# First modulation vectors and sum of squares computed on TensorE instead of VectorE and GpSimd, and six later modulation pieces issued at other places

## The chip, the cores and the metric

The kernel runs on one core of one Trainium2 chip. The core has five engines with their own instruction streams: PE (TensorE, matrix products), ACT (ScalarE), DVE (VectorE), POOL (GpSimd) and SP (SyncE, which here only issues loads and stores). They meet at semaphores. The metric is the time of one execution on the device, in microseconds (us), lower is better.

## The reference

Two small transformer blocks of two layers each run on one sequence `x` of 256 tokens with 1024 features. What the change touches is the start of the first layer: a condition vector `c` gives six modulation vectors, and the first two of them shift and scale the normed input.

```python
mod = jax.nn.silu(c) @ ada_w + ada_b                    # c (1, 1024), ada_w (1024, 6144)
sh_m, sc_m, gt_m, sh_f, sc_f, gt_f = jnp.split(mod[:, None, :], 6, axis=-1)
h = rms_norm(x, norm_mix) * (1 + sc_m) + sh_m
(aq, ak, av, bq, bkc, bvc, ..., cqkv, cz, ca, cb) = jnp.split(h @ w_in, points, axis=-1)
o_a = banded_attention(...)                             # four heads, window 128
o_b = nsa_mixer(...)                                    # compressed, selected and window branches
o_c = gated_delta_net(...)                              # short convolution, then a scan over chunks
x = x + gt_m * (jnp.concatenate([o_a, o_b, o_c], axis=-1) @ w_out)
h = rms_norm(x, norm_ffn) * (1 + sc_f) + sh_f
gate, up = jnp.split(h @ w_gate_up, 2, axis=-1)
x = x + gt_f * ((silu(gate) * up) @ w_down)
```

`rms_norm` divides each token by the root of its mean square, so it needs a sum of squares over all 1024 features of a token.

## The kernel before

Activations lie feature-major: `x` is a tile of 128 partitions by 8 feature blocks (k = 0 to 7) by 256 tokens. Every product with a weight is done as three products in a reduced 32-bit type. `cut` (L188) splits a weight tile into a high part `wh` (a cast on ACT, L193) and a low part `wl` (a subtraction, L194, on DVE or on POOL where `eng` says so). The activations are split in the same way into `hh` and `hl`, and `mm3` (L207 to 211) issues high by high, low by high and high by low.

`begin0` (L452) is the start. It loads `c` and `x`, spreads `c` over all partitions by a product with ones (`cb`, L465), and squares the eight blocks of `x` on ACT (L65) while POOL adds the squares up (L67, one chain of seven). Two products with a column of ones then give the sums (`nps`, L81), `rstd` and `spread` turn them into `rb`, a tile that holds 1/rms of each token on every partition (two products, L272, and a copy, L472). Then four steps j follow. Each takes two modulation units (`mod_unit`, L339), splits one weight block of 512 KB, norms two feature blocks and adds the products that have become possible into four results `pf`.

A modulation unit loads 1 MB, two rows of 1024 weights per partition; DVE multiplies each with the spread silu(c) and sums it (L346), adds the bias (L349) and, for a scale, multiplies the norm's gain in (L352). Units 0 to 3 are the shift, 4 to 7 the scale: eight units, sixteen sums. `norm` (L298) does, for each feature block, `h` = x times `rb` on POOL (L303), scale and shift on ACT (L305), a cast on ACT (L308) and `hl` on POOL (L309).

Units 8 to 23 of layer 0 wait in `pump_list`. `pump(n)` (L355) takes n of them off at fixed places in `mixer1` (L498), in the order of the program. Weights and units come through one ring of three buffers (tag "ws"; `begin0` has five of its own for units), and all their loads stand in the one queue of SP, in order. A load whose buffer is not free holds up all loads behind it.

In `mixer1` the results of the first four blocks go into the convolution, then come `pm`, the query and key blocks, the solve of the delta net, the compression, the loop over `aq` blocks, weight blocks 4 to 7 (`conv(4, ...)`), the loop over `bq` blocks, weight blocks 8 to 11, the gate product `pz`, and the scan (`gdn_scan`), whose first product is `qp`.

Of the kernel before, what the change touches and what calls it, by code (L numbers as in the profile page):

```python
# [17 lines left out]
P = 128  # L18
S = 256
# [123 lines left out]
class Net:  # L143
# [307 lines left out]

    def begin0(self, w_fm, pp):  # L452

        nc, tc, io = self.nc, self.tc, self.io
        with tc.tile_pool(name="st", bufs=1) as sp:
            row = sp.tile([1, 1024], F32, name="row")
            nc.sync.dma_start(row, io["c"])
            nc.sync.dma_start(self.x, io["x"])
            nc.sync.dma_start(self.adab, io["ada_b"])
            nc.sync.dma_start(self.nrm, io["norms"])  # L460
            nc.sync.dma_start(self.cw, io["gdn_conv_w"])
# [10 lines left out]
            nc.scalar.copy(self.rb[:, 0:S], self.spread(self.rcol, (pp, "s", 2)))  # L472
            out = [self.pj.tile([P, S], F32, tag="pj", name="pf") for _ in range(2)]
            out += [pp.tile([P, S], F32, tag="g", name="pf", bufs=3) for _ in range(2)]
            w = []
            for j in range(4):
                for u in (4 + j, j):
                    self.mod_unit(0, u, sp)
                w.append(self.cut(self.load(w_fm[j], (P, KT, P)), eng=nc.gpsimd if j < 3 else None))
                self.norm((2 * j, 2 * j + 1), self.gmod[:, 0, 0, :], self.mod[:, 0, 0:8], range(8), range(8), range(8))  # L480
                for b, (wh, wl) in enumerate(w):
                    for k in range(2 * j if b < j else 0, 2 * j + 2):
                        self.mm3(out[b], wh[:, k, :], wl[:, k, :], self.hh[k][:, 0:S], self.hl[k][:, 0:S],
                                 k == 0, k == KT - 1)
# [13 lines left out]
    def mixer1(self, l, begin, turn):  # L498
        nc, tc, io = self.nc, self.tc, self.io
        with ExitStack() as ctx:  # L500
# [7 lines left out]
            def flush():  # L508
                while late:
                    late.pop(0)()  # L510

            def conv(i0, blocks):
                for j, ps in enumerate(blocks):
# [3 lines left out]
                    if j % 2:  # L517
                        self.pump((3 if i0 == 4 and j == 1 else 1) if l == 0 and i0 > 2 else 0)
# [77 lines left out]
            for blk in range(2):  # L596
# [9 lines left out]
                self.pump(2 if l == 0 else 0)  # L606
# [5 lines left out]
            for blk in range(2):  # L612
# [3 lines left out]
                for br in range(2):  # L616
# [7 lines left out]
                    values()  # L624
                self.split(ot, oh[2 + blk], ol[2 + blk])
# [4 lines left out]
            for tb in range(2):  # L630
# [3 lines left out]
                nc.vector.scalar_tensor_tensor(sz, th, 1.0, pz[tb], op0=ALU.add, op1=ALU.mult)  # L634
            flush()
# [905 lines left out]
```

## Time and profile before

| | |
|---|---|
| median of three runs | 1495.06 us (1493.93 to 1495.86) |
| the profiled execution | 1493.44 us, of which its span 1491.6 |
| PE busy | 1415.6 us (95%) |
| DVE busy | 1139.8 us (76%) |
| ACT busy | 829.5 us (56%) |
| POOL busy | 161.7 us (11%) |
| read from memory | 277.97 MB |

Busy times are of single engines and overlap. Between slices of the span they differ: PE is at 90% or more in most of the 40 slices, and lower in the first (20%), the second (80%) and the fourth (70%). The times in the rows below count from the start of the span.

### The profile page before, as it was taken

Reading aid. Unit: us, or ns where it says so; the run is one execution under the profiler, and the core shown is the slowest. Engines: PE = TensorE matmul, PEld = TensorE weight load, DVE = VectorE, ACT = ScalarE, POOL = GpSimd, SP = SyncE. Lnnn points to the kernel's source line nnn. Section 1 sums busy time; section 2 is a strip of 40 time slices with the busy share of each in tenths; the row PEclk is TensorE's granted clock in tenths of the full one; section 3 lists DMA queues with packets and bytes.
Section 4 is the critical chain, followed back from the end, with each engine's and each line's share of the span. In section 5 each row is a group of like instructions: output and inputs, shape, how many; then the busy total and the mean of one; then the engine's idle time right before and its main releaser. Section 6 shows DMA issues by size and latency. Waiting matters only on the chain.

```text
span 1491.6 us, 29203 instructions
## 1 busy us (share of the span) xinstructions
PE 1415.6 (95%) x11770; PEld 1323.3 (89%) x11770; DVE 1139.8 (76%) x2329; ACT 829.5 (56%) x1591; POOL 161.7 (11%) x156
## 2 busy tenths in 40 slices
PE   2897999999998999999999999999999999999998
PEld 1875788999997788999999888889999888899997
DVE  6868889999967576975667885697888665888875
ACT  3634675544465486654446554575555654755554
POOL 6431201000032300100001011110000100100000
PEclk9998999999999999999999999999999999999999
DMA  8556547888933432779744443279663332655520
GB/s 328 189 210 212 210 167 281 338 323 329 326 108 107 161 123 86 276 265 164 285 162 148 142 142 141 87 284 219 252 234 139 117 117 82 245 215 201 188 85 29
DMA packets 52504, 287.77 MB, mean 193 GB/s; under 512 B 6061, under 2 KB 12081, under 8 KB 24466
## 3 DMA queue, kind: packets, MB, share of 16 engines
q1 hardware_dynamic: 50962, 279.62, 51.4%
q0 software_dynamic: 1408, 6.29, 3.5%
q8 instruction: 92, 1.51, 0.4%
q14 instruction: 42, 0.34, 0.1%
HBM read 277.97 MB, written 7.34 MB: 191 GB/s over the span
## 4 chain that ended last, share of the span: by engine, by line
PE 78%; DVE 11%; POOL 4%; ACT 3%; issue 3%; DMA 1%; POOLq 0%; SPq 0%; DVEq 0%; ACTq 0%
PE pf L209 15%; PE pf L210 14%; PE pf L211 14%; PE acc L209 5%; PE acc L211 5%; PE acc L210 5%; PE sc L379 2%; DVE wl L194 2%; PE ot L422 2%; PE tp L415 1%; POOL sq L67 1%; DVE hl L205 1%; DVE ws L346 1%; PE zp L803 1%; ACT wh L193 1%
## 5 line engine op out<-in xcount | busy, mean ns | idle before, releaser
L209 PE MATMUL pf<-hh,wh 128*128 128x256 f32 (+1 forms) x2008 | 576.0, 288 | 12.9 <-ACT wh L193 6.4
L210 PE MATMUL pf<-hl,wh 128*128 128x256 f32 (+1 forms) x2008 | 574.4, 286 | 11.9 <-DVE hl L205 7.2
L211 PE MATMUL pf<-hh,wl 128*128 128x256 f32 (+1 forms) x2008 | 571.4, 285 | 9.5 <-POOL wl L194 9.2
L193 ACT CAST wh<-ws 128x1024 fp32r<-128x1024 f32 (+1 forms) x303 | 311.3, 1036 | 186.1 <-PE pf L210 131.6
L194 DVE TENSOR_TENSOR wl<-ws,wh 128x1024 fp32r<-128x1024 f32 (+1 forms) x290 | 350.9, 1212 | 78.9 <-ACT wh L193 75.9
L209 PEld LDWEIGHTS pf<-hh,wh 128*128 128x128 f32 x2008 | 384.4, 192 | 22.6 <-issue 7.1
L210 PEld LDWEIGHTS pf<-hl,wh 128*128 128x128 f32 x2008 | 385.0, 192 | 18.9 <-DVE hl L205 10.7
L211 PEld LDWEIGHTS pf<-hh,wl 128*128 128x128 f32 x2008 | 384.0, 191 | 12.1 <-POOL wl L194 9.8
L211 PE MATMUL acc<-ah,dl 128*128 128x256 f32 x704 | 198.2, 282 | 0.0
L210 PE MATMUL acc<-al,dh 128*128 128x256 f32 x704 | 198.0, 282 | 0.0
L209 PE MATMUL acc<-ah,dh 128*128 128x256 f32 x704 | 197.7, 283 | 0.2
L194 DVE TENSOR_TENSOR dl<-wd,dh 128x1024 fp32r<-128x1024 f32 x88 | 107.5, 1222 | 50.0 <-ACT dh L193 49.7
L193 ACT CAST dh<-wd 128x1024 fp32r<-128x1024 f32 x88 | 91.9, 1048 | 94.4 <-PE acc L210 89.2
L67 POOL TENSOR_TENSOR sq<-sq 128x256 f32<-128x256 f32 x59 | 49.2, 834 | 782.6 <-ACT sq L65 776.6
L210 PEld LDWEIGHTS acc<-al,dh 128*128 128x128 f32 x704 | 133.8, 190 | 0.2
L211 PEld LDWEIGHTS acc<-ah,dl 128*128 128x128 f32 x704 | 133.6, 190 | 0.0
L209 PEld LDWEIGHTS acc<-ah,dh 128*128 128x128 f32 x704 | 132.9, 190 | 0.7 <-ACT ah L201 0.6
L346 DVE SCALAR_TENSOR_TENSOR ws<-ws,sc 128x1024 f32<-128x1024 f32 x96 | 119.2, 1255 | 4.7 <-DMA ws<-in_ada_w 4.7
L1093 DVE SCALAR_TENSOR_TENSOR fy<-fu,cw,fy 128x255 f32<-128x255 f32 (+1 forms) x176 | 83.9, 480 | 5.7 <-ACT fy L1091 3.0
L194 POOL TENSOR_TENSOR wl<-ws,wh 128x1024 fp32r<-128x1024 f32 x13 | 34.5, 2652 | 243.9 <-ACT wh L193 239.4
L1074 DVE TENSOR_TENSOR a<-pf,rb 128x258 f32<-128x258 f32 x88 | 37.1, 423 | 30.4 <-PE pf L211 28.8
L395 ACT ACTIVATE lg<-lg,st 128x128 f32<-128x128 f32 x112 | 49.9, 448 | 18.7 <-DVE st L390 14.7
(359 smaller groups left out, 2165.4 us busy)
## 6 DMA issues: line engine op xcount, KB each, us to landing
ws<-in_ada_w SPq DMA_DIRECT2D x48, 1024.0 KB, 6.8
ws<-in_w_gu SPq DMA_DIRECT2D x44, 1024.0 KB, 5.8
wd<-in_w_dn SPq DMA_DIRECT2D x44, 1024.0 KB, 6.2
ws<-in_w_up SPq DMA_DIRECT2D x44, 1024.0 KB, 4.9
ws<-in_w_fm SPq DMA_DIRECT2D x16, 1024.0 KB, 5.0
ws<-in_w_even SPq DMA_DIRECT2D x12, 1024.0 KB, 4.9
w<-in_cmp_w SPq DMA_DIRECT2D x8, 1024.0 KB, 4.9
ws<-in_w_out SPq DMA_DIRECT2D x8, 1024.0 KB, 4.7
```

Of the source, the lines that this page charges most:

```text
L67: (nc.vector if i else nc.gpsimd).tensor_tensor(sq, sq, last, op=ALU.add)
L193: nc.scalar.copy(wh, ws)
L194: (eng or nc.vector).tensor_tensor(wl, ws, wh.bitcast(F32), op=ALU.subtract)
L209: mm(out, lhsT=lh, rhs=rh, start=start, stop=False, **kw)
L210: mm(out, lhsT=lh, rhs=rl, start=False, stop=False, **kw)
L211: mm(out, lhsT=ll, rhs=rh, start=False, stop=stop, **kw)
L346: nc.vector.scalar_tensor_tensor(a, a, 1.0, self.sc, op0=ALU.mult, op1=ALU.mult, accum_out=acc)
L379: self.nc.tensor.matmul(sc[half][:, out], lhsT=q[r, t], rhs=k[r, 0:n], start=True, stop=True)
L395: nc.scalar.activation(lg[:, rng[i]], lg[:, rng[i]], AF.Exp, bias=nm[:, i:i + 1], scale=-1.0, accum_out=den[:, i:i + 1])
L422: mm(out, lhsT=v0, rhs=pt[:, 0:256], start=start, stop=False, skip_group_check=True)
L1074: nc.vector.tensor_tensor(t[j], ps[j], self.rb, op=ALU.mult)
L1093: nc.vector.scalar_tensor_tensor(y[:, d:S], u[:, 0:S - d], w[:, 2 - d:3 - d], y[:, d:S], op0=ALU.mult, op1=ALU.add)
```

## The change

Three things change. First, shift and scale of the first norm: the weights come in another layout (`ada_q`, eight pieces of 1 MB, piece k with the columns of shift block k and scale block k). For a piece, `mod_rows` runs eight fp32 products whose stationary side is a feature block of silu(c), padded with zeros to 32 columns (`cz`), and whose moving side is 256 columns of weights. They go into four strips of 32 partitions of one PSUM tile, two products to a strip. ACT copies the tile, and `mod_cols` sums the strips and turns the row into columns by two products with a single moving column of ones. DVE then adds the bias and multiplies the gain, ACT and DVE make `hh` and `hl` from `xr` = x times `rb`, which is on DVE too. POOL has no part in it any more, and all four weight blocks are cut on ACT and DVE. Three dummy products with ones stand in the tiles of pieces 1 and 2, before the real ones overwrite them.

Second, the sum of squares: ACT squares eight blocks into `xr`, and sixteen products with one moving column each, accumulating in PSUM, replace POOL's chain and the two products behind it.

Third, the pump: conv(4) takes one unit instead of three at its second block, the `aq` loop takes none instead of two in each of two rounds, and instead the `bq` loop takes one unit after each of four pairs, and the `pz` loop one in each of two rounds. Six units move.

```diff
+    def mod_rows(self, sp, pp, k, cz):
+        aw = self.load(self.io["ada_q"][k], (P, KT, 256), sp, tag="aq", bufs=5)
+        ps = pp.tile([P, 256], F32, tag="go"[k % 2], name="mrow", bufs=(3, 1)[k % 2])
+        for _ in range((0, 3, 3)[k] if k < 3 else 0):
+            nc.tensor.matmul(ps, lhsT=self.ones, rhs=cz.rearrange("p k n -> p (k n)"), start=True, stop=True)
+        for i in range(KT):
+            q = slice(32 * (i % 4), 32 * (i % 4) + 32)
+            nc.tensor.matmul(ps[q, :], lhsT=cz[:, i, :], rhs=aw[:, i, :], start=i < 4, stop=i >= 4,
+                             skip_group_check=True)
+        row = sp.tile([P, 256], F32, tag="mrow", name="mrow", bufs=2)
+        nc.scalar.copy(row, ps)
+        return row
+    def mod_cols(self, sp, pp, k, row, xr):
+        mp = pp.tile([P, 2], F32, tag="s", name="mcol")
+        for i in range(2):
+            nc.tensor.matmul(mp[:, i:i + 1], lhsT=row[:, i * P:i * P + P], rhs=self.one, start=True, stop=True)
...
+        nc.vector.tensor_tensor(two(self.mod), mp, two(self.adab), op=ALU.add)
...
+        nc.scalar.activation(hh, xr[:, k, :], AF.Identity, scale=gain, bias=shift)
+        nc.vector.tensor_scalar(h, xr[:, k, :], gain, shift, op0=ALU.mult, op1=ALU.add)
+        nc.vector.tensor_tensor(hl, h, hh.bitcast(F32), op=ALU.subtract)
     def begin0(self, w_fm, pp):
...
-            t = Turn(self, (pp, "s", 2))
+            xr = sp.tile([P, KT, S], F32, name="xr")
+            ms = pp.tile([P, 2], F32, tag="s", name="nps")
             for k in range(KT):
-                t.step(k)
-            t.finish()
-            self.rcol = self.rstd(t.ms)
+                nc.scalar.activation(xr[:, k, :], self.X[k], AF.Square)
+                for tb in range(2):
+                    nc.tensor.matmul(ms[:, tb:tb + 1], lhsT=xr[:, k, tb * P:tb * P + P], rhs=self.one,
+                                     start=k + tb == 0, stop=k == KT - 1, skip_group_check=True)
+            self.rcol = self.rstd(ms)
             nc.scalar.copy(self.rb[:, 0:S], self.spread(self.rcol, (pp, "s", 2)))
+            rows = [self.mod_rows(sp, pp, 0, cz)]
...
-            for j in range(4):
-                for u in (4 + j, j):
-                    self.mod_unit(0, u, sp)
-                w.append(self.cut(self.load(w_fm[j], (P, KT, P)), eng=nc.gpsimd if j < 3 else None))
-                self.norm((2 * j, 2 * j + 1), self.gmod[:, 0, 0, :], self.mod[:, 0, 0:8], range(8), range(8), range(8))
+            for k in range(KT):
+                nc.vector.tensor_tensor(xr[:, k, :], self.X[k], self.rb[:, 0:S], op=ALU.mult)
+                self.mod_cols(sp, pp, k, rows.pop(), xr)
+                if k in (0, 1, 3, 4):
+                    w.append(self.cut(self.load(w_fm[len(w)], (P, KT, P))))
+                if k + 1 < KT:
+                    rows.append(self.mod_rows(sp, pp, k + 1, cz))
                 for b, (wh, wl) in enumerate(w):
...
+            nc.sync.dma_start(self.cw, io["gdn_conv_w"])
     def mixer1(self, l, begin, turn):
...
-                        self.pump((3 if i0 == 4 and j == 1 else 1) if l == 0 and i0 > 2 else 0)
+                        self.pump(1 if l == 0 and i0 > 2 else 0)
...
                 values()
-                self.pump(2 if l == 0 else 0)
                 self.split(ot, oh[blk], ol[blk])
...
                     values()
+                    self.pump(1 if l == 0 else 0)
                 self.split(ot, oh[2 + blk], ol[2 + blk])
...
                 nc.vector.scalar_tensor_tensor(sz, th, 1.0, pz[tb], op0=ALU.add, op1=ALU.mult)
+                self.pump(1 if l == 0 else 0)
```

The order in which TensorE gets its work at the start, up to the two products that make `rb`, follows as a piece of the difference of the two programs. `cb` and `nps` are the spread of `c` and the sums of squares, `mrow` the products of a modulation piece (with `aq`) or the dummies (with `ones`).

```order
-L465 MATMUL cb<-row,ones 128x512 x2
-L81 MATMUL nps<-one,sq 128x1 x2
+L1589 UNCONDITIONAL_BRANCH
+L502 MATMUL cb<-row,ones 128x512 x2
+L510 MATMUL nps<-one,xr 128x1 x6
+L460 MATMUL mrow<-cz,ones 128x256
+L510 MATMUL nps<-one,xr 128x1 x2
+L460 MATMUL mrow<-cz,ones 128x256 x2
+L510 MATMUL nps<-one,xr 128x1 x8
+L463 MATMUL mrow<-aq,cz 32x256 x8
+L460 MATMUL mrow<-cz,ones 128x256 x3
 L272 MATMUL rb<-d,ones 128x128 x2
```

Two `nps` products have become sixteen, and three dummies, the eight products of the first piece and three more dummies have come in ahead of `rb`.

The loads in SP's queue from the compression to the gate product, in the kernel before. The loads of `w_fm` are of block pairs 4, 6, 8 and 10 in this order, and each `ada_w` load is one modulation unit.

```order
L185 DMA ws<-in_ada_w 128x2048 x2
L185 DMA ws<-in_w_fm 128x2x1024
L185 DMA ws<-in_ada_w 128x2048 x7
L185 DMA ws<-in_w_fm 128x2x1024
L185 DMA ws<-in_ada_w 128x2048
L185 DMA ws<-in_w_fm 128x2x1024
L185 DMA ws<-in_ada_w 128x2048
L185 DMA ws<-in_w_fm 128x2x1024
L185 DMA ws<-in_ada_w 128x2048
L185 DMA ws<-in_w_z 128x2048 x2
L185 DMA ws<-in_w_out 128x2048 x4
```

The same stretch of SP's queue in the changed kernel:

```order
L185 DMA ws<-in_ada_w 128x2048 x2
L185 DMA ws<-in_w_fm 128x2x1024
L185 DMA ws<-in_ada_w 128x2048
L185 DMA ws<-in_w_fm 128x2x1024
L185 DMA ws<-in_ada_w 128x2048 x5
L185 DMA ws<-in_w_fm 128x2x1024
L185 DMA ws<-in_ada_w 128x2048
L185 DMA ws<-in_w_fm 128x2x1024
L185 DMA ws<-in_ada_w 128x2048
L185 DMA ws<-in_w_z 128x2048 x2
L185 DMA ws<-in_ada_w 128x2048 x2
L185 DMA ws<-in_w_out 128x2048 x4
```

The load of blocks 6 and 7 has moved ahead of six units, the load of blocks 8 and 9 ahead of two, and two units have come to stand behind the gate's weights.

## Rows read from the trace of the kernel before

**Rows 1.** the page's chain that ended last, shares of the span

```profile
PE 78%; DVE 11%; POOL 4%; ACT 3%; issue 3%; DMA 1%; POOLq 0%; SPq 0%; DVEq 0%; ACTq 0%
```

**Rows 2.** windows: length, busy of PE, PEld, DVE, ACT, POOL, PEclk, DMA, GB/s

```profile
2.00:22.00 20.00, 5.98 (x12) 3.01 (x12) 8.12 (x18) 7.75 (x17) 9.46 (x10) 1.00 1.00 397
22.00:46.00 24.00, 9.36 (x33) 7.59 (x34) 23.73 (x29) 7.45 (x14) 24.00 (x14) 1.00 0.52 202
...
34.00:39.20 5.20, 4.24 (x18) 3.95 (x18) 5.13 (x8) 0.60 (x1) 5.20 (x5) 1.00 0.34 109
...
130.00:157.00 27.00, 17.34 (x93) 13.58 (x91) 23.40 (x72) 13.09 (x41) 2.61 (x1) 0.68 0.58 215
...
170.00:202.00 32.00, 31.45 (x201) 24.83 (x200) 22.22 (x67) 28.32 (x76) 2.40 (x1) 1.00 0.43 151
```

**Rows 3.** chain of waits, 0 to 130 us: start, us, what

```profile
6.73 0.62 ACT sq L65 x2
...
18.46 3.31 POOL h L303 x2
...
43.30 2.44 POOL hl L309 x2
45.78 0.58 PE pf L210
```

**Rows 4.** groups, 0 to 62 us: xcount | busy, mean ns | idle before

```profile
L346 DVE SCALAR_TENSOR_TENSOR ws<-ws,sc 128x1024 f32<-128x1024 f32 x16 | 22.0, 1408 | 3.6 <-DMA ws<-in_ada_w 3.6
...
L194 POOL TENSOR_TENSOR wl<-ws,wh 128x1024 fp32r<-128x1024 f32 x3 | 10.0, 3324 | 0.0
```

**Rows 5.** loads, 0 to 40 us: GB/s in slices of one microsecond

```profile
GB/s 0 4 123 393 418 360 361 394 393 418 401 397 463 426 426 426 422 401 430 434 426 418 418 397 430 434 410 426 418 389 348 57 16 0 0 181 353 31 0 0
```

**Rows 6.** timeline of PE, 130 to 158 us: start, us, instruction, [idle before]

```profile
142.38 0.73 PE L710 MATMUL vp<-ident,cv 128*128 128x128 f32 x2 [0.24 <-ACT vs L711]
149.40 0.58 PE L209 MATMUL pf<-hh,wh 128*128 128x256 f32 x1 [6.29 <-ACT wh L193]
```

**Rows 7.** timeline of SP's queue of loads, 100 to 160 us

```profile
104.60 29.97 SPq L185 DMA_DIRECT2D ws<-in_ada_w  x7
143.55 0.38 SPq L185 DMA_DIRECT2D ws<-in_w_fm  x1
```

**Rows 8.** timeline of PE and PEld, single products at four places

```profile
4.19 1.91 PE L465 MATMUL cb<-row,ones 1*128 1x512 f32 x2
...
13.86 0.93 PEld L81 LDWEIGHTS nps<-one,sq 128*128 128x128 f32 x4 [9.34 <-POOL sq L67]
...
61.69 1.39 PE L722 MATMUL ssp<-one,csq 128*128 128x1 f32 x12
...
97.11 0.62 PE L953 MATMUL hp<-w,win 128*15 128x256 f32 x8
```

**Rows 9.** timeline of PE, weight products, 50 to 56 us

```profile
50.22 0.41 PE L210 MATMUL pf<-hl,wh 128*128 128x256 f32 x1
50.43 0.39 PE L211 MATMUL pf<-hh,wl 128*128 128x256 f32 x1
...
51.48 0.28 PE L211 MATMUL pf<-hh,wl 128*128 128x256 f32 x1
51.60 0.28 PE L209 MATMUL pf<-hh,wh 128*128 128x256 f32 x1
...
55.61 0.29 PE L234 MATMUL pm<-wh,hh 128*128 128x276 f32 x1
```

**Rows 10.** timeline of DVE, one operation of 128 by 256

```profile
108.30 0.41 DVE L817 TENSOR_TENSOR xx<-xx,zp 128x256 f32<-128x256 f32 x1
```

**Rows 11.** chain of waits, 104 to 262 us

```profile
142.38 2.29 DVE ws L346 x4
...
156.64 1.22 DVE wl L194
...
201.38 1.89 PE qp L850 x16
```

More of the change, by code (lines that the diff above doesn't have):

```diff
@@ L449, in out_proj @@
             turn.done()
+    def mod_rows(self, sp, pp, k, cz):
+        nc = self.nc
+        aw = self.load(self.io["ada_q"][k], (P, KT, 256), sp, tag="aq", bufs=5)
[10 more added lines that the diff above has]
+    def mod_cols(self, sp, pp, k, row, xr):
+        nc = self.nc
+        mp = pp.tile([P, 2], F32, tag="s", name="mcol")
+        for i in range(2):
+            nc.tensor.matmul(mp[:, i:i + 1], lhsT=row[:, i * P:i * P + P], rhs=self.one, start=True, stop=True)
+        two = lambda t: t[:, 0, 0:16].rearrange("p (a b) -> p a b", a=2)[:, :, k]
+        nc.vector.tensor_tensor(two(self.mod), mp, two(self.adab), op=ALU.add)
+        shift, gain = self.mod[:, 0, k:k + 1], self.gmod[:, 0, 0, k:k + 1]
+        nc.vector.scalar_tensor_tensor(gain, self.mod[:, 0, 8 + k:9 + k], 1.0, self.nrm[:, N_MIX + k:N_MIX + k + 1],
+                                       op0=ALU.add, op1=ALU.mult)
+        hh, hl = self.hh[k][:, 0:S], self.hl[k][:, 0:S]
+        h = self.np.tile([P, S], F32, tag="h", name="h", bufs=2)
+        nc.scalar.activation(hh, xr[:, k, :], AF.Identity, scale=gain, bias=shift)
+        nc.vector.tensor_scalar(h, xr[:, k, :], gain, shift, op0=ALU.mult, op1=ALU.add)
+        nc.vector.tensor_tensor(hl, h, hh.bitcast(F32), op=ALU.subtract)
     def begin0(self, w_fm, pp):
@@ L472, in begin0 @@
+            self.rcol = self.rstd(ms)
             nc.scalar.copy(self.rb[:, 0:S], self.spread(self.rcol, (pp, "s", 2)))
+            rows = [self.mod_rows(sp, pp, 0, cz)]
+            nc.sync.dma_start(self.adab, io["ada_b"])
+            nc.sync.dma_start(self.nrm, io["norms"])
             out = [self.pj.tile([P, S], F32, tag="pj", name="pf") for _ in range(2)]
             out += [pp.tile([P, S], F32, tag="g", name="pf", bufs=3) for _ in range(2)]
[L475 to L484 removed]
+            w, done = [], [0] * 4
@@ new lines, in begin0 @@
+            for k in range(KT):
[5 more added lines that the diff above has]
+                    rows.append(self.mod_rows(sp, pp, k + 1, cz))
+                for b, (wh, wl) in enumerate(w):
+                    for i in range(done[b], k + 1):
+                        self.mm3(out[b], wh[:, i, :], wl[:, i, :], self.hh[i][:, 0:S], self.hl[i][:, 0:S],
+                                 i == 0, i == KT - 1)
+                    done[b] = k + 1
```

11 lines of the change are left out of this document (8 added, 3 removed).

## The prediction, written before the changed kernel was run

> **What bounds the kernel now.** I read the shares of the chain first, then windows over the first 202 us (the only stretch that the change touches), then the chain inside them, then single rows for prices. Over the whole span the chain is 78% TensorE [rows 1], so a gain must come from a place where TensorE waits. The windows show two such places [rows 2]. In 2 to 22 and 22 to 46 us TensorE is busy 5.98 of 20 and 9.36 of 24 us, while POOL is busy 24.00 of the second 24. In 130 to 157 it is busy 17.34 of 27 us at a granted clock of 0.68; there VectorE (DVE) is busy 23.40 of 27.
>
> The first place is the POOL chain. It takes over at 18.46, when the spread 1/rms (`rb`) exists, and hands back to TensorE at 45.78 after the last `hl` [rows 3]. Each feature pair costs it two products `h`, two `hl` and, for three of the four, a subtraction `wl` of 3.3 us, 10.0 in all; DVE does 16 modulation sums beside it, 22.0 us [rows 4]. All loads from 3 us on flow at about 410 GB/s and are over by 31 us [rows 5], so the transfers do not set this end.
>
> The second place is one wait: TensorE's last product before it starts at 142.38, the next is the first `pf` of block 6 at 149.40, after 6.29 us of waiting for the weights' high part [rows 6]. The load of these weights is issued at 143.55, behind seven modulation loads that sit in SP's queue from 104.60 on [rows 7], each waiting for one of three buffers that DVE must free with two sums.
>
> **Part A, the start.** Removed: POOL's chain, 27.3 us from 18.46 to 45.78 [rows 3], and DVE's 16 sums. Added on TensorE, counted in products:
>
> - 16 single-column products of sums of squares. The four records of the old two took 0.93 us at the slow clock [rows 8], so 0.47 each, 7.4 in all. They start when the first square exists, about 7.3 (it starts at 6.73, two take 0.62 [rows 3], and a wait between engines is on top), so they alone end at 14.7, much where the old ones ended (13.86 + 0.93).
> - Six dummy products of 256 columns. `cb`, 512 columns, took 1.91 [rows 8]; half is 0.95 each, 5.7 in all; three stand among the squares' products and three before the `rb` products.
> - Eight times eight products with 32 stationary columns. The nearest row is `hp`, four strips of 15 columns by 256: eight records (four products) in 0.62 with the last one's tail [rows 8]. One full product of 256 columns would be 0.48 at that clock (half of the dummy's 0.95), so the strips overlap, and eight products cost 1.1 to 1.24 at the fast clock; I take 1.1, without the tail, and twice that at the slow one: 8.8 in all if fast.
> - 16 single-column products of the column turn. At the fast clock 12 records took 1.39 including the last one's tail, so about 0.2 for two records: 3.3 in all [rows 8].
>
> The 96 `pf` products stay. They start 0.21 apart before 50.5 and 0.12 apart after [rows 9]: the slow level (1.2 GHz) and the fast one (2.4 GHz). The granted-clock column reads 1.00 in both windows, so here the level is read off the pitch. At the fast one they cost 11.3.
>
> *When `rb` exists.* Before: 18.4. Now the squares' products with three dummies end between 14.7 and 17.6; the first modulation product and three more dummies (2.5 fast, 5.1 slow) stand ahead of the `rb` products. Ends: 18 and 24. In the kernel before the pitch halved at 50.6, in work that had been unbroken from 45.78; the new order gives such work from about 7.3, so I take 20, nearer the fast end. *From there* TensorE has 3.3 + 7.7 (seven modulation products) + 11.3 = 22.3 us at the fast clock, which gives 42.3 without a stall. Each pair is a chain over four engines (copy on ACT, turn, two small DVE operations, `hh` on ACT, `h` and `hl` on DVE at 0.41 each [rows 10]); TensorE's other pairs cover most of it. I add 3 for stalls and 2 to 3 for a stretch at the slow clock: the last `pf` at about 48 instead of 55.6, where `pm` follows it [rows 9]. *The transfers' floor:* `x`, eight pieces of 1 MB and four weights of half that, 11.6 MB, at 410 GB/s from 3 us on is 31.2 for the eighth modulation piece, or up to 4 more, since its loads stand on SP behind the fourth weight load, which waits for DVE's first `wl`; and about 5 for the chain behind it: 36 to 41, so hidden. DVE has 8 x (0.41 x 3 + 0.3) + 4 x 1.22 = 17 us there, hidden under TensorE's 28; ACT, busy 7.75 and 7.45 us in the first two windows [rows 2], has room for its copies. Behind the start the chain is mostly TensorE's [rows 1], so an earlier end passes on. Gain A: 7.5 us, with ends 2 (`rb` at 24 and the slow clock half the way) and 12 (`rb` at 18, no slow stretch).
>
> On the single columns: the Trainium skill's "TensorEngine Tiling (Array Packing)", section Performance Considerations, gives each matmul about 60 cycles whatever its columns below that; by it the 32 records of the squares' products would take 32 x 50 ns = 1.6 us at 1.2 GHz. The trace has 0.93 for four records, all of it weight load, which is 7.4; the row decides, and the page's figure would only move the early end of `rb`.
>
> **Part B, 104 to 202 us.** Six pumped modulation pieces move behind the `bq` loop and the `pz` loop. SP's order of loads shows it: block 6's weights now follow one modulation load rather than seven, and block 8's follow six rather than eight. So the wait of 6.29 goes from block 6, and something is late next: block 8, whose `wl` on DVE was at 156.64 [rows 11]. What DVE must do before it is what it did before, less the two pieces that now come later, four sums at 2.29 / 2 = 1.14 [rows 11], 4.6 us. In 130 to 157 DVE was idle 27 - 23.40 = 3.6 [rows 2]; if the earlier weights fill that, block 8's `wl` is at 156.64 - 3.6 - 4.6 = 148.4. From there to the first product of the scan (`qp`, 201.38 [rows 11]) TensorE was nearly unbroken (31.45 of 32 us in 170 to 202), and DVE with 22.22 of 32 has 9.8 us for the four sums that come late [rows 2]. So `qp` is 8 us earlier. Ends: TensorE's loss in 130 to 157 is 27 - 17.34 x 0.68 = 15.2, of which at most 14 goes if all of it closes; and 2, if the wait for block 8 grows to nearly what block 6's was. The constants' load for the convolution moves behind the eighth modulation piece; its first reader comes after the last `pf`, 10 us on: nothing, and if late, under 1.
>
> **Sum.** 7.5 + 8 = 15.5. The profiled execution took 1493.44, 1.84 above its span of 1491.6; minus 15.5 that is 1478. The median of the runs is 1495.06, 1.6 above the profiled one: 1479.5.
>
> **Rivals.**
>
> *The slow clock holds through the start (slower).* If the pieces of TensorE's new work come with gaps, the pitch stays at 0.21 all through. Then `rb` is at 24, and from it 2 x 22.3 = 44.6 more: the last `pf` at 68.6, 13 us after 55.6; if a third runs fast, 11 us. For it: in 34 to 39.2 us TensorE was busy 4.24 of 5.2 and the pitch was still 0.21 at 50 [rows 2, 9], and at 0.68 granted in 130 to 157 breaks cost the clock [rows 2]. Against it: the new order has no long break planned, and dummies stand in the breaks. With Part B at its low end the time is 1495.06 + 11 - 2 = 1504; with 8 it is 1498. It is slower from the point where the last `pf` ends after about 66. Chance 0.11. The Trainium skill's "TensorE: Matmul & The Clock Gate", Part 1, says that the slow level is the default and that activity releases it; the halving at 50.6 agrees, and by that rule the rival stands or falls with the breaks.
>
> *The wait only moves.* Block 8 waits as block 6 did, since five modulation loads now stand before its load, and Part B gives nothing. For it: DVE's 23.40 of 27 is nearly full. Against: two pieces do come later. 1495.06 - 7.5 = 1487.5. Chance 0.15.
>
> *The start becomes bound by transfers.* TensorE is fast from 12 us on, no stalls show, and the last `pf` ends at 40: A is 15.5, the time 1471.5. For it: the floor of 36 to 41; against: 22.3 us of work behind `rb` leave no room for that unless `rb` comes by 16. Chance 0.08.
>
> *The change doesn't do what it says: strips run one after another.* Then eight products cost 8 x 0.48 = 3.8 rather than 1.1, 7 x 2.7 = 19 us more, of which some 5 lie in stalls: A is -6.5, the time 1493.6. Against it stands the `hp` row [rows 8]. Chance 0.03.
>
> **How the numbers follow.** The forecast's case has 0.63: 1479.5, its own range 1469 to 1491 (4 and 26 us of gain). The other cases on the faster side end inside or near it. I take 1468 to 1491; outside lie most of the slow-clock rival and of the strips, and little else. About 0.2% (3 us) can be told from no change, so faster is below 1492.1, slower above 1498.0. Faster: 0.60 of the forecast's 0.63, 0.14 of the moved wait, 0.08: 0.82. Same: 0.03 + 0.01, the strips' 0.03, and 0.02 of the slow-clock rival with a full Part B: 0.09. Slower: the other 0.09 of the slow clock.
>
> **What would show it.** Right: POOL idle from 8 to 46 us; `rb` copied at 18 to 24; the eighth modulation load landed by 37; `mrow` groups of eight products in 1.1 to 1.3; the last `pf` at 46 to 50 and its pitch at 0.12 before 30; block 6's `pf` with no wait above 2 us; a new wait at block 8; `qp` at 183 to 190. Wrong: a pitch of 0.21 past 45, `mrow` groups above 2.5, `rb` after 25, a wait of 6 us or more at block 8, or `qp` less than 4 us earlier than the start alone explains; then the step that failed is, in this order, the clock, the strips, the squares, DVE's order, or the two pieces that come late.

## The result, and the profile of the changed kernel

The changed kernel takes 1505.77 us (median of 4 runs, 1501.75 to 1506.91), the one before 1495.31 (4 runs): 1.0067 of it, 95% interval 1.0046 to 1.0087. It is slower by about 10 us, where 1479.5 had been predicted. The profiled execution took 1501.75, with a span of 1500.0.

The shares of the chain that ended last, from its page (before: [rows 1]):

```profile
PE 80%; DVE 11%; ACT 3%; issue 2%; DMA 2%; POOL 2%; SPq 0%; POOLq 0%; DVEq 0%; ACTq 0%
```

POOL's share has halved, as meant, and TensorE's (PE) has grown. Windows of the changed kernel, with the columns of [rows 2]:

```profile
2.00:22.00 20.00, 18.63 (x84) 13.70 (x88) 1.30 (x7) 8.37 (x17) 0.00 (x0) 1.00 0.99 397
20.00:47.00 27.00, 20.41 (x126) 13.95 (x125) 10.11 (x27) 6.98 (x12) 0.00 (x0) 0.62 0.59 213
30.00:40.00 10.00, 7.29 (x47) 4.52 (x40) 2.41 (x8) 2.89 (x5) 0.00 (x0) 0.50 0.65 238
47.00:63.50 16.50, 14.89 (x135) 11.93 (x136) 6.85 (x20) 5.36 (x11) 0.00 (x0) 1.00 0.20 68
63.50:81.60 18.10, 15.90 (x115) 15.22 (x114) 16.15 (x43) 15.57 (x36) 2.48 (x2) 0.91 0.75 261
154.00:174.00 20.00, 14.00 (x60) 9.82 (x60) 15.98 (x55) 11.33 (x34) 3.21 (x1) 0.66 0.58 207
```

POOL does nothing from 2 to 63.5 us. TensorE idles 6.59 of the 27 us from 20 to 47 and holds a granted clock of 0.62 in them. From the first product of the scan (`qp`, 210.55 here and 201.24 before) to the end of the span the two profiles take 1289.5 and 1290.4 us, so the loss lies ahead of it. TensorE's first 82 us, in the timeline (start, us, instruction, [idle before]):

```profile
18.45 2.21 PE L460 MATMUL mrow<-cz,ones 128*128 128x256 f32 x6
20.50 0.61 PE L272 MATMUL rb<-d,ones 128*128 128x128 f32 x4
21.38 1.07 PE L463 MATMUL mrow<-aq,cz 128*32 128x256 f32 x16
24.01 0.38 PE L209 MATMUL pf<-hh,wh 128*128 128x256 f32 x1 [1.56 <-ACT hh L482]
...
25.61 0.28 PE L210 MATMUL pf<-hl,wh 128*128 128x256 f32 x1
26.83 0.58 PE L209 MATMUL pf<-hh,wh 128*128 128x256 f32 x1 [0.94 <-ACT hh L482]
27.99 0.58 PE L211 MATMUL pf<-hh,wl 128*128 128x256 f32 x1 [0.58 <-DVE wl L194]
28.37 0.41 PE L209 MATMUL pf<-hh,wh 128*128 128x256 f32 x1
...
29.57 1.94 PE L463 MATMUL mrow<-aq,cz 128*32 128x256 f32 x16
...
34.15 0.79 PE L209 MATMUL pf<-hh,wh 128*128 128x256 f32 x2 [1.08 <-ACT hh L482]
35.12 1.94 PE L463 MATMUL mrow<-aq,cz 128*32 128x256 f32 x16
...
42.16 1.94 PE L463 MATMUL mrow<-aq,cz 128*32 128x256 f32 x16
...
47.49 0.28 PE L210 MATMUL pf<-hl,wh 128*128 128x256 f32 x1
...
49.84 1.07 PE L463 MATMUL mrow<-aq,cz 128*32 128x256 f32 x16
...
59.85 0.38 PE L234 MATMUL pm<-wh,hh 128*128 128x276 f32 x1
...
63.37 0.28 PE L211 MATMUL pf<-hh,wl 128*128 128x256 f32 x1
...
69.68 0.39 PE L209 MATMUL pf<-hh,wh 128*128 128x256 f32 x1 [2.20 <-ACT wh L193]
...
81.65 1.88 PE L727 MATMUL dp<-ug,cs 128*128 128x512 f32 x4
```

The reader sees the fast level from 21 (eight products in 1.07 us), its loss at 26.8 behind waits of 1.56 and 0.94 for `hh` (products of 0.28 become 0.41 and eight cost 1.94), and its return at 47.3. The pieces' products from 29.57 to 49.84 stand 5.6 to 7.7 us apart. The last `pf` starts at 63.37, and `pm`, which followed it in the kernel before at 55.61 [rows 9], is mixed with it. `dp` opens the next stage: 81.65, against 70.87 before.

The loads, GB/s in slices of 1 us from 0 to 40, flow as in [rows 5] except for a break at 22 to 24, and are nearly over at 38:

```profile
GB/s 0 4 119 254 410 426 410 459 335 456 422 442 377 459 418 426 442 410 389 426 438 426 33 16 283 283 319 295 336 369 434 188 180 229 377 353 424 129 55 13
```

### The profile page after: what moved, and what is told of

The parts are those of the page before. It is cut to its first block, busy times and chain, and to the rows that moved or that the text cites. A ratio compares the mean times of both kernels' runs of the same rounds, so it can differ in the third digit from the quotient of the medians.

```text
span 1500.0 us, 29580 instructions
## 1 busy us (share of the span) xinstructions
PE 1444.7 (96%) x11970; PEld 1340.7 (89%) x11970; DVE 1122.4 (75%) x2329; ACT 830.5 (55%) x1592; POOL 126.6 (8%) x130
## 3 DMA queue, kind: packets, MB, share of 16 engines
q0 software_dynamic: 1408, 6.29, 3.5%
## 4 chain that ended last, share of the span: by engine, by line
PE 80%; DVE 11%; ACT 3%; issue 2%; DMA 2%; POOL 2%; SPq 0%; POOLq 0%; DVEq 0%; ACTq 0%
PE pf L209 15%; PE pf L211 15%; PE pf L210 15%; PE acc L209 5%; PE acc L211 5%; PE acc L210 5%; PE sc L379 3%; DVE wl L194 2%; PE ot L422 2%; PE tp L415 1%; DVE hl L205 1%; PE zp L852 1%; PE pv L234 1%; PE pv L235 1%; PE pv L236 1%
## 5 line engine op out<-in xcount | busy, mean ns | idle before, releaser
L67 POOL TENSOR_TENSOR sq<-sq 128x256 f32<-128x256 f32 x52 | 44.1, 849 | 779.1 <-ACT sq L65 773.6
L346 DVE SCALAR_TENSOR_TENSOR ws<-ws,sc 128x1024 f32<-128x1024 f32 x80 | 96.7, 1218 | 1.5 <-DMA ws<-in_ada_w 1.5
L1140 ACT ACTIVATE fy<-fu,cw 128x256 f32<-128x256 f32 x88 | 52.6, 599 | 12.1 <-DVE fu L1139 11.8
```

The source lines that it names most:

```text
L67: (nc.vector if i else nc.gpsimd).tensor_tensor(sq, sq, last, op=ALU.add)
L346: nc.vector.scalar_tensor_tensor(a, a, 1.0, self.sc, op0=ALU.mult, op1=ALU.mult, accum_out=acc)
L1140: nc.scalar.activation(y, u, AF.Identity, scale=w[:, 2:3], bias=w[:, 3:4])
```

## The experiments

The landmarks in all of them are the starts of `dp` (end of the first stage) and `qp` (the scan's first product, behind all that the change touches). In before they are at 70.87 and 201.24, in the changed kernel at 81.65 and 210.55. The stretch behind `qp`, in which the kernels differ little, takes 1285.7 to 1293.9 us in the fourteen profiles, so a landmark tells more than a total. Still, each landmark comes from one execution, and not always from a typical one: the profiled execution is the fastest of its kernel's runs in the changed kernel, `e5`, `e8` and `e11`, the slowest in `e1` and the second slowest in `e12`. A start can repeat within 0.1 us (`dp` at 70.83 to 70.89 in before, `e1`, `e7` and `e8`; 81.65 and 81.58 in the changed kernel and `e2`), or not: `e5` and `e10` have the same start and `dp` at 63.88 and 65.84.

**Each half alone.** `e1` has the moved pieces with the old start, `e2` the new start with the old pump. `e1`:

```diff
-                        self.pump((3 if i0 == 4 and j == 1 else 1) if l == 0 and i0 > 2 else 0)
+                        self.pump(1 if l == 0 and i0 > 2 else 0)
...
-                self.pump(2 if l == 0 else 0)
...
+                    self.pump(1 if l == 0 else 0)
...
+                self.pump(1 if l == 0 else 0)
```

> The kernel before with its old start and only the six modulation pieces moved. Theory: in the changed kernel the stretch from the first `dp` product to `qp` took 128.9 us against 130.4 before, so the move of the pieces is worth 1 to 2 us and this kernel takes about 1493.5. Rival: the move is worth the 8 us that were predicted, and the late start of the changed kernel hid it; then this kernel takes about 1487.

`e2` undoes the same lines in the changed kernel:

```diff
-                        self.pump(1 if l == 0 and i0 > 2 else 0)
+                        self.pump((3 if i0 == 4 and j == 1 else 1) if l == 0 and i0 > 2 else 0)
...
+                self.pump(2 if l == 0 else 0)
...
-                    self.pump(1 if l == 0 else 0)
...
-                self.pump(1 if l == 0 else 0)
```

> The changed kernel with its new start and the six modulation pieces back at their old places. Theory: the start alone is 10.8 us late at the first `dp` product, and all of it reaches the end: about 1506. Rival: the loss comes from the pieces that pile up later, and the start's lateness is taken up by waits that exist anyway: about 1498.

Measured: `e1` 1489.46 us, 0.9975 of before [0.9959, 0.9991], `dp` 70.88, `qp` 199.13. `e2` 1503.26, 1.0079 [1.0053, 1.0104], `dp` 81.58, `qp` 211.90. As the theory of both had it, the whole loss is the new start's, and the moved pieces gain about 2 us at `qp`, where 8 were predicted.

**Is it the clock?** `e3` fills TensorE's waits behind the first four turns with four dummy products each.

```diff
-    def mod_cols(self, sp, pp, k, row, xr):
+    def mod_cols(self, sp, pp, k, row, xr, scratch, cz):
...
+        for _ in range(4 if k < 4 else 0):
+            nc.tensor.matmul(scratch, lhsT=row[:, 0:P], rhs=cz.rearrange("p k n -> p (k n)"), start=True, stop=True)
```

> The changed kernel with four more dummy products of 256 columns behind each of the first four column turns, where TensorE waits for ACT and DVE; 16 in all, whose results are overwritten. Clock theory: the waits of 0.3 to 1.6 us between 24 and 28 us let the granted clock fall at 26.8, and the half-speed stretch to 46.9 costs about 10 us; with the waits filled the clock stays up, the pairs follow each other 3.3 us apart as they did after 50, the last `pf` ends near 52 and the whole takes about 1495. Chain theory: what sets the start is the chain mrow, copy, turn, DVE, ACT, DVE of each pair, at any clock; then the dummies add up to 7.5 us of work at the fast clock (0.47 each) and the time is 1505 to 1512.

Measured: 1496.61, 1.0031 [1.0014, 1.0047]; `dp` 76.06, `qp` 204.20. Its window from `rb` to its last `pf`:

```profile
20.00:59.40 39.40, 36.69 (x291) 28.62 (x290) 16.97 (x46) 12.41 (x23) 0.00 (x0) 1.00 0.49 174
```

By the pitch TensorE is slow until 23.9 here (six records of the new dummies, from 21.18 on, take 2.91); from then on the level holds, every later `mrow` group takes 1.07, and 5.6 us come back although 16 products more are done. So keeping TensorE busy and fast gives back half of the loss. The other half, with the price of 22 dummies in it, stays with the level up: the clock is not the whole cause. The last `pf` starts at 59.33, between the 52 of the clock theory and the changed kernel's 63.37.

**One piece further ahead.** `e4` emits the products of two later pieces ahead of a piece's weight products, where the changed kernel has one.

```diff
-        row = sp.tile([P, 256], F32, tag="mrow", name="mrow", bufs=2)
+        row = sp.tile([P, 256], F32, tag="mrow", name="mrow", bufs=3)
...
+            rows.append(self.mod_rows(sp, pp, 1, cz))
...
-                self.mod_cols(sp, pp, k, rows.pop(), xr)
+                if k + 2 < KT:
+                    rows.append(self.mod_rows(sp, pp, k + 2, cz))
+                self.mod_cols(sp, pp, k, rows.pop(0), xr)
```

> The changed kernel with the modulation products of a piece issued two pieces ahead instead of one (three row buffers instead of two), no further dummies. In the changed kernel the third piece's products started at 29.6 though its load had been issued at 5.3 to 7 and others behind it had landed. Chain theory: the copies and turns then lie under the products of earlier pairs, TensorE waits less, and the last `pf` ends 8 to 10 us earlier: about 1496. Clock theory: the first waits, around 24 us for the first `hh` and `wl`, stay, the clock falls again, and only the waits themselves (3 to 4 us) are saved: about 1501.

Measured: 1507.22, 1.009 [1.0064, 1.0116]; `dp` 78.24, `qp` 213.91. Its third group of products came forward to 23.64 (29.57 in the changed kernel), but the next two still stood behind weight products, at 30.09 and 37.62: the scheduler that sets the order of the queue had put them back. In between TensorE waited 1.58 us for a `wl` and ran slow again. The 3.4 us won at `dp` were lost twice over behind it (from `dp` to `qp` 135.7 us, 128.9 in the changed kernel); why stays open. So this is no clean test of the idea, and the next kernels write the order down.

**The order written down.** `e5` makes the weight products of piece k wait, in the order of issue, for the products of piece k + 3, issues the loads of five pieces and two weight blocks at the start, puts the fourth block's products behind those of the other three, and has nine dummies among the turns instead of the six ahead of `rb`.

```diff
+            for what in (la, la, la, lw, la, lw, la):
+                what()
...
-                for b, (wh, wl) in enumerate(w):
+                with tc.issue_after(ends[min(k + LA, KT - 1)].ins):
+                    for b, (wh, wl) in enumerate(w):
+                        if b == 3 and k < KT - 1:
+                            continue
```

> The changed kernel with the order of TensorE's queue at the start written down: the products of a modulation piece stand three pieces ahead of the weight products that need them, modulation pieces are loaded before the third and fourth weight block, blocks 3 and 4 come last, and nine dummies stand behind the third to fifth column turn. Order theory: in the changed kernel the third piece had landed long before its products ran at 29.6; with the pieces ahead, TensorE has 22.3 us of products and 4.2 us of dummies behind `rb` and DVE 17, so the last `pf` ends at 46 to 50, the first `dp` comes at about 66 to 69 instead of 81.7, and the time is about 1492 or less. Clock theory: if the clock falls in spite of that, between 24 and 30 us, the last `pf` ends at 55 to 60 and the time is 1500 or more.

Measured: 1488.76, 0.9971 [0.9956, 0.9986]; `dp` 63.88, `qp` 192.51. The start is now 7 us earlier than that of the kernel before, as the order theory had it, but four edits did it. `e6` takes one of them by itself: `e3` with the fourth block last.

```diff
-                for b, (wh, wl) in enumerate(w):
+                for b, (wh, wl) in enumerate(w[:3]):
...
+            with tc.issue_after(end.ins):
+                for i in range(KT):
+                    self.mm3(out[3], w[3][0][:, i, :], w[3][1][:, i, :], self.hh[i][:, 0:S], self.hl[i][:, 0:S],
+                             i == 0, i == KT - 1)
```

> The run with 16 dummies again, but the fourth weight block's 24 products come after all others instead of among them, as in the kernel before. In the run with the dummies the clock stayed up, and yet the first `dp` came 20.3 us after the first `pm` (before: 15.3). Ring theory: six pairs of cut weights exist, four are held by the four blocks until the eighth piece, so the casts for `pm` wait (1.7 us at ACT) and then collide with the convolution of four blocks; with the fourth block last, three pairs come free first, and `dp` is at 72 to 74 instead of 76.1: about 1493 to 1494. Rival: the convolution's own work on ACT and DVE sets that stretch; then `dp` stays at 76 or later and the time at 1496.6 or more.

Measured: 1494.88, 1.0022 [1.0007, 1.0038]; `dp` 75.82, `qp` 204.69. It gives nothing at `dp` (76.06 in `e3`), so the forecast of 72 to 74 missed. The waits it was meant for did go: from the first `pm` to `dp` TensorE is busy 19.64 of 19.95 us, where `e3` has 14.40 of 16.60 from 59.4 to 76.0. But in the start the fourth block's products had been filling waits, and without them TensorE idles 5.7 us from 20 to 59.4 instead of 2.7. The waiting has moved from behind the start into it.

`e9` is `e5` without its nine dummies, `e11` the changed kernel without its six, `e12` is `e9` with the fourth block beside the others again.

```diff
-        for _ in range(3 if scratch is not None else 0):
+        for _ in range(0 if scratch is not None else 0):
```

> The run with the written-down order, without its nine dummies. Order theory: the pieces ahead of the weight products do the work; the dummies cost up to 9 x 0.47 = 4.2 us and without them the last `pf` ends at 45 to 49, `dp` comes at 61 to 65 (with them 63.9), the time is 1485 to 1489. Clock theory: without them the waits for the first `hh` and `wl` at 20 to 25 us keep or bring TensorE to the slow pitch, the last `pf` ends after 54 and `dp` comes after 69: 1494 or more.

```diff
-        for _ in range((0, 3, 3)[k] if k < 3 else 0):
+        for _ in range(0):
```

> The changed kernel without the six dummies of its start. Clock theory: without them TensorE has less unbroken work ahead of `rb`, reaches the fast pitch later or not before 45, and though `rb` comes up to 3 us earlier the last `pf` ends at 64 or later: 1506 or more. Rival: the dummies only delay `rb` (5.7 us at the slow clock, 20.5 instead of 18) and the clock falls at 26.8 all the same; then the last `pf` comes 2 to 3 us earlier and the time is about 1503.

```diff
-                        if b == 3 and k < KT - 1:
-                            continue
```

> The written order without dummies (e9), but the fourth block's products stand in their place beside the other three again instead of behind them; all else as in e9. If the order of the pieces (three ahead of the weight products) is what repaired the start, the last pf of the start still ends near 48 to 56 us with the fast pitch from about 33 on, and only the stretch behind it pays: pm to dp takes about 20 rather than 15.2 us, dp starts at 66 to 69 and the time is within 3 us of e9's 1483.4. If putting the fourth block last was the repair, the start falls back to that of the changed kernel: last pf near 60, dp at 75 or later, time at or above before's, 1494 or more. If both share it, dp lies at 70 to 74.

Measured: `e9` 1483.42, 0.9936 [0.9915, 0.9957], `dp` 63.94, `qp` 193.64; `e11` 1499.24, 1.0036 [1.0019, 1.0053], `dp` 77.72, `qp` 206.65; `e12` 1487.68, 0.9982 [0.9963, 1.0000], `dp` 70.71, `qp` 203.68. These make a ladder at `dp`: 81.65 in the changed kernel, 77.72 without its dummies, 70.71 with the order written down, 63.94 with the fourth block last too. `e9` is faster than both kernels, and the order theory named its `dp`; `e11` came out faster than either of its two forecasts, since `rb` came 4.9 us earlier and not 2 to 3; `e12` lies where its forecast has both edits share the repair. The rung between `e11` and `e12` is the one that decides; the windows of `e11`, then of `e12`:

```profile
18.00:44.00 26.00, 20.06 (x118) 13.04 (x107) 10.15 (x27) 6.61 (x11) 0.00 (x0) 0.61 0.66 252
44.00:59.50 15.50, 14.08 (x129) 11.33 (x130) 6.31 (x18) 5.29 (x11) 0.00 (x0) 1.00 0.22 75
```

```profile
20.00:44.00 24.00, 23.51 (x148) 15.11 (x149) 10.28 (x30) 8.06 (x15) 0.00 (x0) 1.00 0.58 235
44.00:52.60 8.60, 8.60 (x75) 8.60 (x75) 4.79 (x9) 4.12 (x8) 0.00 (x0) 1.00 0.55 191
```

From 18 us to its last `pf` TensorE idles 5.94 + 1.42 = 7.4 us in `e11`; in `e12` it is 0.5 in the window and as much from 18 to 20, 1.0 in all. The difference of 6.4 is most of the 7.0 at `dp`. The clock is not in this rung: both are slow until nearly the same time, `e11` (after a fast spell from 20.0 to 22.8) until 43.3 and `e12` until 43.9. `e12` shows it by the pitch, whatever the clock column says:

```profile
15.72 1.22 PE L272 MATMUL rb<-d,ones 128*128 128x128 f32 x4
...
32.63 1.94 PE L458 MATMUL mrow<-aq,cz 128*32 128x256 f32 x16
36.93 1.94 PE L458 MATMUL mrow<-aq,cz 128*32 128x256 f32 x16
41.23 1.94 PE L458 MATMUL mrow<-aq,cz 128*32 128x256 f32 x16
...
43.70 0.41 PE L211 MATMUL pf<-hh,wl 128*128 128x256 f32 x1
...
44.06 0.50 PE L469 MATMUL mcol<-one,mrow 128*128 128x1 f32 x4
```

(`e12` also has its loads earlier in SP's queue and more row buffers than `e11`; these were not tried apart from the order. In `e11` no idle time of an engine between 14 and 60 us is put down to a load, which speaks for the order.)

The rung from `e12` to `e9`, 6.8 us, is only in part the fourth block's. Up to the turn of the eighth piece both do the same work in the same order, and up to 34 us at the same times. `e9`:

```profile
32.65 1.94 PE L458 MATMUL mrow<-aq,cz 128*32 128x256 f32 x16
36.01 1.07 PE L458 MATMUL mrow<-aq,cz 128*32 128x256 f32 x16
...
40.13 0.61 PE L469 MATMUL mcol<-one,mrow 128*128 128x1 f32 x4
```

`e9` is fast from 34.9 on, `e12` from 43.9, and the same turn comes at 40.13 and at 44.06: 3.9 us of the rung are TensorE's level, in two single executions. They are there nearly in full at the first `pm` (48.78 and 52.60); the other 2.9 us lie between `pm` and `dp`, where the edit acts.

So a start without waits still pays for the slow level, but dummies did not buy a better one. `e5`, with nine of them, ends as `e9` does:

```profile
20.29 1.07 PE L458 MATMUL mrow<-aq,cz 128*32 128x256 f32 x16
...
22.86 2.91 PE L471 MATMUL pf<-cz,mrow 128*128 128x256 f32 x6
```

It was fast at 20.29, ahead of its first dummy, slow in the first three dummies and fast from 25.9 on; its nine dummies take some 6.0 us, and that and what the level gives back come out even.

**The moved pieces.** `e1`, `e7` and `e8` share the old start. In TensorE's timeline of `e1`, waits of over 0.4 us from 140 to 157:

```profile
142.07 0.33 PE L711 MATMUL vp<-ident,cv 128*128 128x128 f32 x1 [0.65 <-DVE cv L705]
142.85 0.33 PE L711 MATMUL vp<-ident,cv 128*128 128x128 f32 x1 [0.46 <-ACT vs L712]
144.66 0.33 PE L711 MATMUL vp<-ident,cv 128*128 128x128 f32 x1 [1.48 <-DVE cv L705]
146.23 0.58 PE L209 MATMUL pf<-hh,wh 128*128 128x256 f32 x1 [0.45 <-ACT wh L193]
149.80 0.47 PE L711 MATMUL vp<-ident,cv 128*128 128x128 f32 x1 [2.56 <-DVE cv L705]
150.73 0.48 PE L711 MATMUL vp<-ident,cv 128*128 128x128 f32 x1 [0.46 <-ACT vs L712]
151.81 0.39 PE L1012 MATMUL ctp<-ident,ce 128*64 128x128 f32 x1 [0.60 <-DVE ce L1011]
```

They sum to 6.7 us: the one wait of 6.29 for a weight block [rows 6] has become seven, of which 4.7 us are for DVE's convolution (`cv`). DVE in the same execution, and POOL's only cut in that stretch:

```profile
144.19 0.42 DVE L705 SCALAR_TENSOR_TENSOR cv<-cu,cv 128x256 f32<-128x256 f32 x1
...
146.04 1.22 DVE L346 SCALAR_TENSOR_TENSOR ws<-ws,sc 128x1024 f32<-128x1024 f32 x1
147.19 0.08 DVE L346 DVE_READ_ACCUMULATOR ws<-ws,sc 128x1 f32 x1
147.19 2.56 DVE L705 SCALAR_TENSOR_TENSOR cv<-cu,cv 128x256 f32<-128x256 f32 x1
```

```profile
146.25 3.21 POOL L194 TENSOR_TENSOR wl<-ws,wh 128x1024 fp32r<-128x1024 f32 x1 [26.02 <-ACT wh L193]
```

The operation that takes 0.42 alone takes 2.56 when POOL cuts weights beside it, and TensorE's longest wait (2.56, at 149.80) is for it. `e7` takes these cuts from POOL:

```diff
-            conv(4, (ps for i in (4, 6) for ps in self.blocks(w_fm, i, pool=(1,), ws=ws.get(i))))
+            conv(4, (ps for i in (4, 6) for ps in self.blocks(w_fm, i, ws=ws.get(i))))
...
-            conv(8, (ps for i in (8, 10) for ps in self.blocks(w_fm, i, pool=(1,))))
+            conv(8, (ps for i in (8, 10) for ps in self.blocks(w_fm, i)))
```

> The run with only the six pieces moved, with the weight cuts of blocks 5, 7, 9 and 11 of both layers on DVE instead of POOL. In that run a convolution operation on DVE took 2.56 us instead of 0.41 at 147.2, while POOL ran its cut, and TensorE waited for it 2.56 us. Port theory: DVE is held while POOL works, so taking POOL's cut away saves these 2 us and costs DVE 1.2 for the cut: 0 to 1 us faster here for each, 1486 to 1489 if the one without is 1488. Rival: DVE is the bound of that stretch, four more cuts of 1.2 in each layer cost 2 to 5 us: 1490 or more.

`e8` moves two more pieces behind the gate product:

```diff
-                        self.pump(1 if l == 0 and i0 > 2 else 0)
+                        self.pump(1 if l == 0 and i0 > 4 else 0)
...
-                self.pump(1 if l == 0 else 0)
+                self.pump(2 if l == 0 else 0)
```

> The run with only the six pieces moved, with the two pieces of blocks 4 to 7 moved on to the gate product as well. Theory: what TensorE waits for between 142 and 152 in that run is DVE's convolution operations with four modulation sums of 1.14 us between them; without these sums the waits (6.9 us in all) go down by 3 to 4.6 and the clock falls later or not at all: `qp` 4 to 6 us earlier, the time about 1484. Rival: the wait moves on once more, to blocks 8 to 11 or behind the gate product, where the sums now stand: within 2 us of 1488.

Measured: `e7` 1490.01, 0.9984 [0.9971, 0.9997], `qp` 195.86; `e8` 1490.57, 0.9985 [0.9969, 1.0000], `qp` 193.55. In one profile each, `qp` is 3.3 and 5.6 us earlier than in `e1`; the medians show none of it, so neither improves on `e1` as far as can be told. (`e8`'s profile is of its fastest run, `e1`'s of its slowest.) In `e7` all eight `cv` operations of this form take 0.42, so the port theory is right about the operation, and the wait of 2.56 is gone, and 1.71, 1.22 and 1.51 stand nearby; in `e8` they have moved to `ctp` (1.85) and `tp` (2.06). `e10` joins `e5` and the later pieces of `e8`; its edit of `e5`:

```diff
-                        self.pump(1 if l == 0 and i0 > 2 else 0)
+                        self.pump(1 if l == 0 and i0 > 4 else 0)
...
-                self.pump(1 if l == 0 else 0)
+                self.pump(2 if l == 0 else 0)
```

> The run with the written-down order, with the two pieces of blocks 4 to 7 moved on to the gate product as in the run with only the pieces moved. Alone the order brought `qp` from 201.2 to 192.5 and the later pieces (with the old start) to 193.6. If the two gains add, `qp` comes at 186 to 188 and the time is 1482 to 1486. Rival: what the runs gain here is given back behind 202 us, where the granted clock differs from run to run: 1488 to 1491 whatever `qp` says.

Measured: 1490.36, 0.9972 [0.9955, 0.9988], `dp` 65.84, `qp` 194.58: no better than `e5`. It was slow until 29.3, 3.4 us longer than `e5`, and is 2.0 us behind it at `dp`; from `dp` to `qp` both take 128.7 us, so the two later pieces gave nothing there.

## Why the prediction was wrong, step by step

**The step that failed** is, in part A, "TensorE's other pairs cover most of it. I add 3 for stalls and 2 to 3 for a stretch at the slow clock". From `rb` (20.50) to the last `pf` (63.37) the changed kernel needs 42.9 us; 27.8 were predicted (22.3 of work, 3 of stalls, 2.5 for the clock). By the windows, 6.59 + 1.61 = 8.2 of it are idle (3 predicted). From 26.8 to 47.3 TensorE is busy 16.69 us at a granted clock of 0.50; half of that, 8.3, is what the clock cost (2.5 predicted; an estimate, which supposes that all this work takes half the time at the fast level). The remaining 26.4 are work at the fast level (22.3 predicted; eleven `pm` products that are mixed in are 1.4 of the difference). The difference of the two programs already showed why other pairs can't cover: a piece's products are only one piece ahead, so its copy, turn, `hh` and `hl` stand open with few weight products to fill them. More than half of the idle time is for `hh`, and the waits came with the loss of the level at 26.8; that loss was the rival "the slow clock holds through the start", given 0.11. It gave a last `pf` at 66.6 to 68.6 and 1498 to 1504 us; 63.4 and 1505.8 came.

That rival's mechanism was only half right, though. With the level kept (`e3`) half of the loss stays. With six dummies fewer and the waits gone, at the slow level until 43.9 (`e12`), all of it goes: 3.9 + 7.0 us of the 10.8 at `dp`. What made the start later than the old one was waiting inside the piece-by-piece chain, and the dummies ahead of it; the slow level made each turn of the chain longer (eight products 1.94 instead of 1.07), and cost even `e12` 3.9 us against `e9`. The prediction had also taken the fast level to follow where work is unbroken, as at 50.6 in the kernel before; `e12`, with two waits of 0.49 us between 7 and 43.9, was slow all that time, so that reading does not carry over.

**Dummies.** They were priced right (5.7 in all; the trace has 1.20 + 2.05 + 2.21 = 5.5) and placed on the path without a price for what they give: `rb`'s products start at 20.50 with them and at 15.58 without (`e11`), and 3.9 of that arrive at `dp`.

**Behind the start** the prediction said "an earlier end passes on" and had nothing for a later one. From the first `pm` to `dp` the changed kernel takes 21.8 us, before 15.3. All four blocks end together behind the eighth piece, and their convolution meets the casts of the next weights on ACT: TensorE waits 2.20 us for one at 69.68. ACT there:

```profile
62.77 0.65 ACT L193 CAST wh<-ws 128x552 fp32r<-128x552 f32 x1 [1.75 <-PE pm L235]
63.33 0.64 ACT L739 COPY cu<-pf 128x256 f32<-128x256 f32 x2
...
65.99 0.66 ACT L193 CAST wh<-ws 128x552 fp32r<-128x552 f32 x1
66.67 1.28 ACT L752 ACT_TABLE_LOAD   x1
...
68.60 1.03 ACT L193 CAST wh<-ws 128x1024 fp32r<-128x1024 f32 x1
```

The casts come one by one between convolution steps. In `e9`, with the fourth block last, TensorE is busy 15.10 of 15.10 us in that stretch (48.8 to 63.9), and it takes 2.9 us less than in `e12`. In `e6` the same edit took the waits out there too, but they came back in the start. As far as these runs show, the edit pays where the start has no waits left that the fourth block's products were filling.

**What was right.** `rb` was copied at 21.14 (18 to 24 predicted), eight products in strips take 1.07 (1.1), POOL is idle, and the transfers are hidden. The end of the start at 48 that was predicted is reached by the written order (`pm` at 48.78 in `e9`, and `dp` 6.9 us earlier than in the kernel before): the pieces were there, in another order than the one that was run. That it comes so near is partly luck: `e9` has its `rb` products at 15.73 and is slow until 34.9, and the sum had `rb` at 20 and a short slow stretch.

**Part B** said "block 8 waits as late next" and DVE's idle time would fill. The wait of 6.29 did go, but others came in its place. In the changed kernel, where all of this comes some 11 us later, seven waits of 0.15 to 2.57 stand from 153.5 to 163.9, 6.4 us in all, at the convolution's turns and not at block 8. The longest:

```profile
161.87 0.47 PE L759 MATMUL vp<-ident,cv 128*128 128x128 f32 x1 [2.57 <-DVE cv L753]
```

The granted clock is no better behind them: 0.66 from 154 to 174, and in `e1` 0.67 from 140 to 157 (before: 0.68 in 130 to 157 [rows 2]). `e1` has 10 us (140 to 150) in which TensorE is busy 4.12 and DVE 9.06: by these shares the bound there is DVE, which has modulation sums of 1.2 us between the convolution's steps. 8 us were predicted; in `e1` 2.1 came at `qp`, and its ratio of 0.9975 is 3.7 us [1.3 to 6.1]. Of the rivals "the wait only moves" was the nearer one, with another place.

What stays open: how much of the rung from `e11` to `e12` the earlier loads give; what decides when TensorE's level rises, if the same work brings it at 34.9 in one execution and at 43.9 in another; and how much `e9` gains on `e12` in a typical run. That `e5`'s median is 5 us above `e9`'s, with a `qp` no later, says little: its profile is of the fastest of its twelve runs, 8.3 us below their median.

## What to carry to other kernels

Where work moves from a slow engine into a chain that crosses four engines per piece, count how many pieces are open at once in the order that will run, and write that order down if the scheduler puts it otherwise: here 7.0 us of a loss of 10.8 at the next stage went with three ahead instead of one, written down (its loads, too, stood earlier). Products added to keep TensorE fast belong into its waits: six ahead of the product that everything waits for cost 3.9 us, sixteen in the waits gave 5.6 (`e3`), nine in a start that hardly waits gave nothing (`e5` against `e9`). Ask of the engines behind whether a later, more abrupt end collides with their next work. And before a difference between two profiles is put down to an edit, look for the last instruction up to which both did the same work: what they differ by there, the edit did not do.

## What the runs showed of the hardware that was not expected

- TensorE fell to the slow pitch at 26.8 behind waits of 1.56, 0.31 and 0.94 us in 22.4 to 26.8, and stayed slow until 47.3, while busy 7.29 of 10 us (30 to 40). The Trainium skill's "TensorE: Matmul & The Clock Gate", Part 1, has the slow level as the default and activity as what releases it. Activity alone did not do it soon in `e12`: TensorE was busy 23.51 of 24 us from 20 to 44, with 32-column strips, single columns and some full products, and was slow until 43.9; `e9`, with the same work at the same times until 34, was fast from 34.9. So with the same work the level rose 9 us apart, and no run tells what decides.
- The granted-clock column reads 1.00 in that window of `e12` while eight products take 1.94: ahead of the first rise the level has to be read off the pitch, and 0.50 to 0.62 appear only once it has fallen.
- A DVE operation over 128 by 256 that began at 147.19 in `e1` took 2.56 us instead of 0.42 beside a POOL cut that had begun at 146.25. The DVE sum that had begun before the cut, at 146.04, took its usual 1.22, and the cut took 3.21, where the ones before and after it took 2.36 and 2.38.
- Taking such a wait out (`e7`) or moving sums (`e8`) made `qp` 3 to 6 us earlier in one profile and nothing in the medians, while the stretch behind `qp` differs by up to 8 us between profiles: a stage's landmark and the time must both be asked.
